# A two-layer trunk with experts: top two by eight-largest instructions, and a ring of 23 weight matrices opened in steps

## The chip, the cores and the metric

One core of a Trainium2 chip runs the whole kernel: TensorE (PE in the rows), VectorE (DVE), ScalarE (ACT), GpSimd (POOL), and SyncE (SP), whose queue issues every transfer. The metric is the device time of one execution in microseconds (us). The kernel before takes 1189.0 us, the median of three runs (1187.51 to 1193.46).

## The reference

There are two layers on 256 tokens of width 1024, all in float32. Each layer has a mixer sublayer (three token mixers on one input projection, merged by gates, then one output projection and a layer norm) and a mixture of experts. The expert part is what the change is about:

```python
group_logits = xt @ wg + bg
p_group = max(softmax(group_logits)); top_group = argmax(group_logits)
in_group = the 8 expert logits of that group            # 4 groups of 8 experts
top_val, top_idx = lax.top_k(in_group, 2)
w_top = softmax(top_val) * p_group
combine[t, e] = w_top at the two chosen experts, else 0
h_e = silu(x @ w_gate[e]) * (x @ w_up[e])               # 32 experts, each 1024 x 256
moe = sum over e of (h_e * combine[:, e]) @ w_down[e]   # 256 x 1024
h = layer_norm(ALPHA * h + moe)
```

An expert has three matrices of 1 MiB (gate, up, down), so that a layer reads 96 MiB of expert weights.

## The kernel before

**Weights.** `queue_weights` writes out one list of loads, in the order of use. `issue(pool)` takes the next one, gives it a 1 MiB tile (8 KiB in each partition) of a pool and puts its DMA on SP's queue; `done(key)` marks a matrix as used and issues the next load into the same pool. Four such tiles live for the whole kernel (`NBUF`), 13 are opened when the buffers of the mixers close (`NPRE`, `open_prefetch`), and five more (`NMORE`) when everything of the mixer sublayer has closed (`cr.close()`). SP works its queue in order: a load that waits for its tile holds back all behind it. At most eight loads are under way, since each waits for the eighth before it to land.

**The mixer's end.** Pools on the right side of the on-chip memory lie like a stack. The merge pool `gp` holds, among others, the mixers' outputs `o4`; on top lies `x`, with the transposed input `hT`. `merge_branch` works the three branches a, b and c; in the last one `between` closes `x`, opens a pool `out` there and begins to turn the merged result (`mix_turned`). `project_out` multiplies by `w_out` in two halves of 512 columns and starts the router's logits (`route`).

**The router.** `router` normalises, with `norm_scale` finding 1/sqrt by three Newton rounds of small VectorE operations. Beside it TensorE runs 26 multiplications whose result nobody uses (`warm`). Then the two best experts of each token are found: a maximum, an equality, a tie broken by position (`first`, three operations), the found one struck out, and the same again; `sel` is the sum of the two one-hots. Each of these steps is two instructions, one for each block of 128 tokens. Five small multiplications by triangles of ones turn `sel` into the token's place in each expert's list (`pos`), followed by `warm(6)`.

**The experts.** They are worked in quads of four: `QUADS` is 0, 1, 2, "x", 3 to 7, where "x" is a second turn of the expert with most tokens (99 MiB in all). For each quad `tokens` builds a 0/1 matrix `P` from `pos`, eight operations of 32 columns; `gather` multiplies by it and evicts to `xg`; `up` runs all gate and then all up matrices of the quad and calls `done` after each kind; `turn`, `down` and `combine` follow, while `weigh` (on POOL), `slots` and `slots_out` prepare the weights of the slots. `in_turn` keeps TensorE's order as written. Between the first quads POOL also applies the norm's gain and shift to the residual (`scaled`, eight operations); its two rows of 1024 values are broadcast to all partitions by four DMAs, issued before the router.

Of the kernel before, what the change touches and what calls it, by code (L numbers as in the profile page):

```python
# [20 lines left out]
KT = D // 128  # L21
# [43 lines left out]
def host_consts():  # L65
    p = np.arange(128)
    i64 = np.arange(64)
    j = (p % 64)[:, None]
    same = (p[:, None] // 64) == (p[None, :] // 64)
    S = {}  # L70
    S["ident"] = np.eye(128)
    S["rank"] = np.broadcast_to(p[None, :] + 1, (128, XCAP))
    S["down"] = np.broadcast_to(32 - np.arange(32)[None, :], (128, 32))
# [34 lines left out]
class Trunk:  # L108
# [35 lines left out]
    NBUF, NPRE, NMORE = 4, 13, 5  # L144
# [22 lines left out]
    def queue_weights(self):  # L167
        nc, A = self.nc, self.A

        def chunk(l, n):  # L170
            if n[:3] == "br_":
                c0, w, k, src = 512 * int(n[4]), 512, 4, A["w_br_" + n[3]][l]
            elif n[:-1] in WIDE:
                (a, c0), w, k = WIDE[n[:-1]], 512, 4
                src = A[a][l, 512 * int(n[-1]):512 * int(n[-1]) + 512]
            else:
                (c0, w), k, src = CH[n], 8, A["w_in"][l]

            def emit(t):
                return nc.sync.dma_start(t[:, :k * w].rearrange("p (k c) -> p k c", k=k),  # L180
                                         src.rearrange("(k p) c -> p k c", p=128)[:, :, c0:c0 + w])
            return (l, n), emit

        def expert(l, n, e):

            def emit(t):
                if e == "x":
                    src = A[n][l, bass.ds(self.heavy[l], 1)].rearrange("e (p k) f -> p (e k f)", p=128)
                else:
                    src = A[n][l, e].rearrange("(p k) f -> p (k f)", p=128)  # L190
                return nc.sync.dma_start(t, src)
            return (l, n, e), emit

        q, self.heavy = [], {}
        for l in range(DEPTH):
            q += [chunk(l, n) for n in ORDER]
            for quad in QUADS:
                q += [expert(l, n, e) for n in EXPERT for e in experts(quad)]
        self.wq = q[::-1]
        self.issue(self.wp)  # L200

    def issue(self, pool):
        if self.wq:
            key, emit = self.wq.pop()
            t = pool.tile([128, 2048], F32, name="w", tag="w", bufs=self.bufs[pool])
            self.last_weight = emit(t)
            self.wtiles[key] = t, pool
# [97 lines left out]
    def norm_scale(self, st, eps, centre=None):  # L305
# [3 lines left out]
        mv, rs, nm, v, tmp = (self.hp.tile([128, TB, w], F32, name=n, tag=n) for n, w in  # L309
                              (("ln_mv", 2), ("ln_rs", 1), ("ln_nm", 1), ("ln_v", 1), ("ln_tmp", 1)))  # L310
# [260 lines left out]
    def layer(self, l):  # L571
        tc, side = self.tc, dict(side="right")
        with ExitStack() as cl, ExitStack() as cr:
# [4 lines left out]
            hp = xp.enter_context(tc.tile_pool(name=f"x{l}", bufs=1, **side))  # L578
            with tc.tile_pool(name=f"mix{l}", bufs=1) as mp:
# [16 lines left out]
                self.hT = [hp.tile([128, KT, T], F32R, name=n) for n in ("hTh", "hTl")]  # L596
# [29 lines left out]
            po = ExitStack()  # L626

            def between():
                xp.close()
                pool = po.enter_context(tc.tile_pool(name=f"out{l}", bufs=1, **side))  # L630
                self.mixS = [pool.tile([128, 8, T], F32R, name=n) for n in ("mixh", "mixl")]
# [7 lines left out]
            with tc.tile_pool(name=f"h1_{l}", bufs=1, **side) as xp, tc.tile_pool(name=f"moe{l}", bufs=1, **side) as ep:  # L639
                self.moe(l, xp, ep, self.h)  # L640
# [475 lines left out]
    def o4(self, dt=F32R):  # L1116
        return [self.gp.tile([128, 4, T], dt, name="o4", tag="o4", bufs=self.NB["o4"]) for _ in range(2)]
# [156 lines left out]
    def project_out(self, l, po):  # L1274
# [16 lines left out]
        for c in range(2):  # L1291
            ps = [self.ps("pa") for _ in range(TB)]
            for i in range(2):
# [3 lines left out]
                if c == 1 and i == 0:  # L1297
                    for t in range(TB):
                        route(t, 0)
            cs = slice(512 * c, 512 * c + 512)  # L1300
# [8 lines left out]
    def router(self, l, ep, x, xc):  # L1309
# [46 lines left out]
        gm, pen, el, m1, m2, oh1, oh2, f = s(1), s(4), s(32), s(1), s(1), s(32), s(32), s(1)  # L1356
        es = self.small([128, TB, 32])
        for t in both:
            red(gm[t], lg[t][:, 0:4], axis=AX.X, op=OP.max)
# [44 lines left out]
        def heaviest(cmb):  # L1404
# [10 lines left out]
            ts(n, f1, -1.0, 32.0, op0=OP.mult, op1=OP.add)  # L1415
# [74 lines left out]
    def moe(self, l, xp, ep, h1):  # L1490
        nc, A = self.nc, self.A
        self.open_small(ep, 760)
# [16 lines left out]
        def tokens(q):  # L1509
# [3 lines left out]
            for t in range(TB):  # L1513
                if quad == "x":
                    nc.vector.tensor_scalar(P[:, t], rank, heavy[:, t, 0:1], self.rs[:, t], op0=OP.is_equal, op1=OP.mult)
                    continue
# [56 lines left out]
        def up(q):  # L1573
# [10 lines left out]
            if q == 0:  # L1584

                slots(0)
# [14 lines left out]
        def down(q):  # L1601
# [3 lines left out]
            for c in range(2):  # L1605
# [5 lines left out]
                y = [ep.tile([128, 512], F32R, name=n, bufs=2) for n in ("Yh", "Yl")]  # L1611
# [20 lines left out]
        heavy, past = heaviest(cmb)  # L1632
        tokens(1)
        with self.tc.issue_after(self.pool_last.ins):
            self.scaled(h1, *rows, nc.gpsimd)
# [6 lines left out]
        for q in range(nq + 1):  # L1642
            if q == 1:

                self.heavy[l] = nc.values_load(self.heaviest, engines=[mybir.EngineType.SP], min_val=0, max_val=NE - 1)
            if q < nq:
                self.in_turn(up, q)
            if q:
# [8 lines left out]
            if 3 <= q < 7:  # L1657
                c, t = divmod(q - 3, 2)
# [20 lines left out]
        rows = [[ep.tile([128, 512], F32, name=n, tag=n, bufs=2) for _ in range(2)] for n in ("Yh", "Yl")]  # L1679
# [52 lines left out]
```

## Time and profile before

| | us |
|---|---|
| runs: median, lowest, highest | 1189.0, 1187.51, 1193.46 |
| the profiled execution | 1191.11 |
| its span, first to last instruction | 1189.3 |

The profile is of one execution; its span and what lies around it (1.8 us) make up its time. Times in rows count from the first instruction. Layer 0 runs its experts from about 375 to 588 us, layer 1 from about 957 to 1170 us. PE is busy for 90% of the span, DVE 52%, ACT 37%, POOL 15%; 305.57 MB are moved. An engine's share says little here, since the stages have different limits.

### The profile page before, as it was taken

What the parts mean: (1) busy time and instruction counts of PE and PEld (TensorE: products, weight loads), DVE (VectorE), ACT (ScalarE), POOL (GpSimd) and SP (SyncE); (2) the same over time, 40 slices, a digit from 0 to 9 for tenths busy, and PEclk for the clock granted to TensorE, in tenths of its full rate; (3) what the DMA queues carried; (4) which work ended last, traced back from release to release, by engine and by line L of the source; (5) the groups of instructions that cost most, each with busy time, mean ns of one, the idle gap of its engine ahead of it and who ended that gap; (6) DMA issues with size and microseconds to landing.
All of it is one profiled execution on the core that took longest, in us unless ns stands there. A gap on an engine that the chain in (4) does not pass through costs nothing.

```text
span 1189.3 us, 21512 instructions
## 1 busy us (share of the span) xinstructions
PE 1065.1 (90%) x8846; PEld 770.8 (65%) x8846; DVE 615.1 (52%) x1404; ACT 444.8 (37%) x804; POOL 178.3 (15%) x160
## 2 busy tenths in 40 slices
PE   5899998999999899777689999899999999978775
PEld 4788976777777555334378889667777765634342
DVE  7787749366557234221177875665655563422214
ACT  4564553454444122111066545445444341211111
POOL 2411016001210300000024110430021131000001
PEclk9999998999999999888999999999999999997988
DMA  8632331358965999999983224215599579999994
GB/s 230 193 98 66 94 128 36 112 177 317 409 258 224 408 419 418 419 419 419 383 234 103 73 72 132 82 37 160 184 390 397 178 314 419 418 419 420 419 419 181
DMA packets 105282, 305.57 MB, mean 257 GB/s; under 512 B 21026, under 2 KB 48092, under 8 KB 79836
## 3 DMA queue, kind: packets, MB, share of 16 engines
q1 hardware_dynamic: 105180, 304.15, 67.9%
q8 instruction: 71, 1.16, 0.4%
q14 instruction: 31, 0.25, 0.1%
HBM read 303.08 MB, written 1.05 MB: 256 GB/s over the span
## 4 chain that ended last, share of the span: by engine, by line
PE 24%; DMA 15%; DVE 4%; ACT 3%; issue 2%; POOL 1%; SPq 1%; DVEq 0%; POOLq 0%
DMA w<-in_exp_w_gate_dram 5%; DMA w<-in_exp_w_down_dram 5%; DMA w<-in_exp_w_up_dram 3%; PE ps_pa L247 3%; PE ps_pa L246 3%; PE ps_pa L248 3%; PE ps_po L247 2%; PE ps_po L248 2%; PE ps_po L246 2%; DMA Yh<-in_ln_g_dram 2%; ACT wh L234 1%; PE ps_pa L1579 1%; DVE wl L235 1%; PE ps_pb L819 1%; PE ps_pm L1609 1%
## 5 line engine op out<-in xcount | busy, mean ns | idle before, releaser
L235 DVE TENSOR_TENSOR wl<-w,wh 128x1024 fp32r<-128x1024 f32 x150 | 187.9, 1253 | 156.9 <-ACT wh L234 156.1
L234 ACT CAST wh<-w 128x1024 fp32r<-128x1024 f32 x158 | 165.7, 1049 | 199.3 <-PE ps_pa L248 67.0
L1579 PE MATMUL ps_pa<-w,xg 128*32 128x256 f32 x2304 | 174.8, 431 | 60.6 <-DMA w<-in_exp_w_up_dram 35.1
L1579 PEld LDWEIGHTS ps_pa<-w,xg 128*32 128x32 f32 x2304 | 84.1, 123 | 145.8 <-DMA w<-in_exp_w_up_dram 46.3
L1590 DVE SCALAR_TENSOR_TENSOR hm<-ps_pa,ws,hm 128x256 f32<-128x256 f32 x18 | 8.7, 484 | 203.8 <-ACT hm L1589 203.6
L1589 ACT ACTIVATE hm<-ps_pa 128x256 f32<-128x256 f32 x18 | 6.9, 385 | 223.6 <-PE ps_pa L1579 223.6
L1609 PE MATMUL ps_pm<-w,hmT 128*32 128x512 f32 x576 | 70.9, 596 | 2.2 <-issue 1.3
L1529 PEld LDWEIGHTS ps_pm<-P,h1c 128*128 128x128 f32 x576 | 66.9, 192 | 2.9 <-ACT res L1331 1.1
L1529 PE MATMUL ps_pm<-P,h1c 128*128 128x128 f32 x576 | 67.8, 275 | 0.4
L1538 ACT ACTIVATE xg<-ps_pm,gb 128x128 f32<-128x128 f32 x72 | 33.0, 458 | 83.1 <-DVE xg L1536 82.9
L247 PE MATMUL ps_pa<-wl,hTh 128*128 128x512 f32 x144 | 58.5, 406 | 0.9 <-POOL wl L235 0.6
L246 PE MATMUL ps_po<-wh,hTh 128*128 128x512 f32 x144 | 58.2, 404 | 1.0 <-DVE mix L1260 0.6
L247 PE MATMUL ps_po<-wl,hTh 128*128 128x512 f32 x144 | 58.3, 405 | 0.9 <-POOL wl L235 0.6
L246 PE MATMUL ps_pa<-wh,hTh 128*128 128x512 f32 x144 | 58.2, 404 | 1.0 <-DVE mix L1260 0.5
L248 PE MATMUL ps_po<-wh,hTl 128*128 128x512 f32 x144 | 58.1, 404 | 0.0
L248 PE MATMUL ps_pa<-wh,hTl 128*128 128x512 f32 x144 | 57.8, 402 | 0.0
L1551 POOL TENSOR_TENSOR Pw<-P,small 128x128 f32<-128x128 f32 x32 | 12.4, 405 | 298.0 <-PE ps_pm L1558 220.0
L1262 POOL TENSOR_TENSOR mix<-mix,sg 128x512 f32<-128x512 f32 x16 | 28.3, 1788 | 153.0 <-DVE sg L1260 153.0
L246 PE MATMUL ps_pa<-hTh,wh 128*128 128x256 f32 (+1 forms) x168 | 49.4, 294 | 2.0 <-ACT wh L655 2.0
L1536 DVE TENSOR_SCALAR xg<-ps_pm,gb 128x128 f32<-128x128 f32 x72 | 29.5, 409 | 41.4 <-PE ps_pm L1529 32.4
L248 PE MATMUL ps_pa<-hTh,wl 128*128 128x256 f32 (+1 forms) x168 | 49.2, 293 | 0.7 <-DVE wl L235 0.5
L248 PE MATMUL ps_po<-hTh,wl 128*128 128x256 f32 (+1 forms) x168 | 49.1, 292 | 0.5 <-DVE wl L235 0.5
(468 smaller groups left out, 2282.6 us busy)
## 6 DMA issues: line engine op xcount, KB each, us to landing
w<-in_exp_w_gate_dram SPq DMA_DIRECT2D x66, 1024.0 KB
w<-in_exp_w_up_dram SPq DMA_DIRECT2D x66, 1024.0 KB
w<-in_exp_w_down_dram SPq DMA_DIRECT2D x66, 1024.0 KB
w<-in_w_in_dram SPq DMA_DIRECT2D x58, 1024.0 KB
w<-in_w_out_dram SPq DMA_DIRECT2D x8, 1024.0 KB
w<-in_w_br_a_dram SPq DMA_DIRECT2D x4, 1024.0 KB
w<-in_w_br_b_dram SPq DMA_DIRECT2D x4, 1024.0 KB
w<-in_w_br_c_dram SPq DMA_DIRECT2D x4, 1024.0 KB
```

What stands on the lines that cost most here:

```text
L234: nc.scalar.copy(v(hi), raw)
L235: engine.tensor_tensor(v(lo), raw, v(hi).bitcast(F32), op=OP.subtract)
L246: mm(ps, a[0], b[0], start=start, stop=False, skip_group_check=True)
L247: mm(ps, a[0], b[1], start=False, stop=False, skip_group_check=True)
L248: mm(ps, a[1], b[0], start=False, stop=stop, skip_group_check=True)
L1262: nc.gpsimd.tensor_tensor(mv, mv, sg[t], op=OP.add)
L1529: nc.tensor.matmul(ps[:, 128 * k:128 * k + 128], xc[:, t, 4 * h + k], Ps[q][:, t], start=(t == 0), stop=(t == 1))
L1536: nc.vector.tensor_scalar(xg[:, k], o, g, b, op0=OP.mult, op1=OP.add)
L1538: nc.scalar.activation(xg[:, k], o, AF.Identity, scale=g, bias=b)
L1551: self.pool_last = nc.gpsimd.tensor_tensor(e(Pw[:, t]), e(P[:, t]), w, op=OP.mult)
L1579: nc.tensor.matmul(pg[32 * e:32 * e + 32, FF * n:FF * n + FF], xgs[q][k // 4][:, k % 4, 32 * e:32 * e + 32], w[:, FF * k:FF * k + FF], sta ...
L1609: nc.tensor.matmul(ps[32 * e:32 * e + 32], hmT[:, i, 32 * e:32 * e + 32], w[:, D * i + 512 * c:D * i + 512 * c + 512], start=(i == 0), sto ...
```

## The change

1. **Ring.** The five late tiles are opened in steps: two when branch c is merged (`o4` now has a pool of its own, `o`, on top of `x`, that closes first), two after the last multiplication by `w_out` (`free` closes `x`; the turned result now lies in the tiles of `hT`), one at `cr.close()`. One load, the gate matrix of expert 3, is taken out of the list and goes to a tile of its own (`once`), so that 23 matrices fit before the first is used. That tile is not used again for weights: the tiles of `Y` lie there afterwards.
2. **Rows.** The norm's two rows are one entry of the weight list, behind quad 1, and `scaled` is called at quads 2 and "x".
3. **Top two.** `max` gives the eight largest values of a row at once. A score `sc` of one or two values (with the position breaking ties), and a second `max`, replace the two searches; `sel` is one comparison, and the one-hots are made later, in `weights`.
4. **P** is built by two operations of 256 columns in place of eight of 32.
5. **Norm.** The three Newton rounds become one round of third order and one Newton round: nine operations in place of twelve.

```diff
-    NBUF, NPRE, NMORE = 4, 13, 5
+    NBUF, NPRE = 4, 13
+        def rows(l):
+            def emit(t):
+                for i, n in enumerate(("ln1_g", "ln1_b")):
+                    self.bcast_row(t[:, D * i:D * i + D], A[n][l], D)
+            return (l, "rows"), emit
             for quad in QUADS:
                 q += [expert(l, n, e) for n in EXPERT for e in experts(quad)]
+                if quad == 1:
+                    q += [rows(l)]
+            self.once[l] = q.pop(q.index(next(x for x in q if x[0] == (l, EXPERT[0], 3))))
...
-        if pool is self.wp or (self.wq and self.wq[-1][0][0] == key[0]):
+        if pool is self.wp or pool in self.bufs and (self.wq and self.wq[-1][0][0] == key[0]):
...
-        ts(v, v, -0.5, None, op0=OP.mult)
+        ts(v2, v, -0.5 * 27 / 512, None, op0=OP.mult)
...
-        for _ in range(3):
-            for t in range(TB):
-                ts(tmp[:, t], rs[:, t], rs[:, t], v[:, t], op0=OP.mult, op1=OP.mult)
-            for t in range(TB):
-                ts(rs[:, t], tmp[:, t], 1.5, rs[:, t], op0=OP.add, op1=OP.mult)
+        for t in range(TB):
+            ts(tmp[:, t], rs[:, t], rs[:, t], v[:, t], op0=OP.mult, op1=OP.mult)
+        nc.vector.scalar_tensor_tensor(tmp, tmp, -10.0 / 3, tmp, op0=OP.add, op1=OP.mult)
+        for t in range(TB):
+            ts(rs[:, t], tmp[:, t], 5.0, rs[:, t], op0=OP.add, op1=OP.mult)
+        for t in range(TB):
+            ts(tmp[:, t], rs[:, t], rs[:, t], v2[:, t], op0=OP.mult, op1=OP.mult)
+        for t in range(TB):
+            ts(rs[:, t], tmp[:, t], 1.5 * 3 / 8, rs[:, t], op0=OP.add, op1=OP.mult)
...
             self.merge_branch(l, "c", between)
-            with po:
-                self.project_out(l, po)
+            oc.close()
+            self.open_prefetch(f"more{l}a", 2)
+            def free():
+                xp.close()
+                self.open_prefetch(f"more{l}b", 2)
+            self.project_out(l, free)
             cr.close()
-            self.open_prefetch(f"more{l}", self.NMORE)
+            self.open_prefetch(f"more{l}c", 1)
...
         for t in both:
-            red(m1[t], el[t], axis=AX.X, op=OP.max)
-        first(oh1, el, m1, 32)
+            nc.vector.max(top[t], el[t])
+        m1, m2 = ([x[:, i:i + 1] for x in top] for i in range(2))
         for t in both:
-            stt(el[t], oh1[t], -3e38, el[t], op0=OP.mult, op1=OP.add)
+            stt(c[t], el[t], m2[t], down, op0=OP.is_ge, op1=OP.mult)
         for t in both:
-            red(m2[t], el[t], axis=AX.X, op=OP.max)
-        first(oh2, el, m2, 32)
+            stt(sc[t], el[t], m2[t], c[t], op0=OP.is_gt, op1=OP.add)
+        for t in both:
+            nc.vector.max(rank2[t], sc[t])
...
-            tt(sel[:, t], oh1[t], oh2[t], op=OP.add)
+            ts(sel[:, t], sc[t], rank2[t][:, 1:2], None, op0=OP.is_ge)
...
+                for i, oh in enumerate((oh1, oh2)):
+                    ts(oh[t], sc[t], rank2[t][:, i:i + 1], None, op0=OP.is_equal)
...
-        rows = [[ep.tile([128, 512], F32, name=n, tag=n, bufs=2) for _ in range(2)] for n in ("Yh", "Yl")]
-        for r, n in zip(rows, ("ln1_g", "ln1_b")):
-            for c in range(2):
-                self.bcast_row(r[c], A[n][l, 512 * c:512 * c + 512], 512)
+        yp = yc.enter_context(self.tc.tile_pool(name=f"once{l}", bufs=1, side="right"))
+        key, emit = self.once[l]
+        self.wtiles[key] = yp.tile([128, 2048], F32, name="w"), yp
+        emit(self.wtiles[key][0])
...
-                for e in range(4):
-                    i = nc.vector.tensor_scalar(P[:, t, CAP * e:CAP * e + CAP], rank[:, 0:CAP], pos[:, t, 4 * quad + e:4 * quad + e + 1],
-                                            self.rs[:, t], op0=OP.is_equal, op1=OP.mult)
-                    self.last_P = i.ins
+            nc.vector.tensor_tensor(P.rearrange("p t (e s) -> p t e s", s=CAP),
+                                    pos[:, :, 4 * quad:4 * quad + 4, None].to_broadcast([128, TB, 4, CAP]),
+                                    rank[:, None, None, 0:CAP].to_broadcast([128, TB, 4, CAP]), op=OP.is_equal)
+            self.last_P = nc.vector.tensor_tensor(P, P, self.rs.to_broadcast([128, TB, 128]), op=OP.mult).ins
...
-        with self.tc.issue_after(self.pool_last.ins):
-            self.scaled(h1, *rows, nc.gpsimd)
...
+            if q in (2, 3):
+                r = self.w(l, "rows")
+                self.scaled(h1, *([r[:, D * i + 512 * c:D * i + 512 * c + 512] for c in range(2)] for i in range(2)), nc.gpsimd,
+                            [q - 2])
+                if q == 3:
+                    self.done(l, "rows")
```

Three engines get another order. On SP, at the end of layer 0's mixers, this is the queue of loads before, each with the engines or the earlier transfer (DMAHW) that it waits for; it begins with the last load that waits for a tile of `w_out`:

```order
L191 DMA w<-in_exp_w_up_dram 128x2048 [waits DMAHW4_49,DVE_49]
L191 DMA w<-in_exp_w_up_dram 128x2048 [waits DMAHW5_49,PE_49,Activation_49]
L191 DMA w<-in_exp_w_up_dram 128x2048 [waits DMAHW6_49]
L191 DMA w<-in_exp_w_up_dram 128x2048 [waits DMAHW7_49]
L191 DMA w<-in_exp_w_down_dram 128x2048 [waits DMAHW0_49]
L191 DMA w<-in_exp_w_down_dram 128x2048 [waits DMAHW1_49]
L297 DMA Yh<-in_ln_g_dram 128x512 [waits DMAHW2_49]
L297 DMA Yh<-in_ln_g_dram 128x512 [waits DMAHW3_49]
L297 DMA Yl<-in_ln_b_dram 128x512 [waits DMAHW4_49]
L297 DMA Yl<-in_ln_b_dram 128x512 [waits DMAHW5_49]
L191 DMA w<-in_exp_w_down_dram 128x2048 [waits DMAHW6_49,PE_49]
```

And now, from the first of the two tiles that `o4` leaves (a wait for PE) to the rows:

```order
L191 DMA w<-in_exp_w_gate_dram 128x2048 [waits DMAHW1_49,PE_49]
L191 DMA w<-in_exp_w_gate_dram 128x2048 [waits DMAHW2_49]
L191 DMA w<-in_exp_w_up_dram 128x2048 [waits DMAHW3_49,DVE_49]
L191 DMA w<-in_exp_w_up_dram 128x2048 [waits DMAHW4_49,DVE_49]
L191 DMA w<-in_exp_w_up_dram 128x2048 [waits DMAHW5_49,DVE_49]
L191 DMA w<-in_exp_w_up_dram 128x2048 [waits DMAHW6_49,DVE_49]
L191 DMA w<-in_exp_w_down_dram 128x2048 [waits DMAHW7_49,PE_49]
L191 DMA w<-in_exp_w_down_dram 128x2048 [waits DMAHW0_49]
L191 DMA w<-in_exp_w_down_dram 128x2048 [waits DMAHW1_49,PE_49,Activation_49]
L191 DMA w<-in_exp_w_gate_dram 128x2048 [waits DMAHW2_49]
L191 DMA w<-in_exp_w_down_dram 128x2048 [waits DMAHW3_49,PE_49]
L308 DMA w<-in_ln_g_dram 128x1024 [waits DMAHW4_49,PE_49]
```

The five loads that stood together behind the wait for PE and ACT are now two, two and one, the lone gate matrix stands behind them, and the rows come behind the first load that needs a used expert matrix to go.

On DVE, the router of layer 0 before, from the first maximum to `P` (x2: one instruction for each block of tokens):

```order
L1365 TENSOR_REDUCE small<-small 128x1 x2
L1347 SCALAR_TENSOR_TENSOR small<-small,const 128x32 x2
L1349 TENSOR_REDUCE small<-small 128x1 x2
L1352 TENSOR_SCALAR small<-small 128x32 x2
L1368 SCALAR_TENSOR_TENSOR small<-small 128x32 x2
L1370 TENSOR_REDUCE small<-small 128x1 x2
```

It goes on with the same three steps for the second expert, `sel` and `pos`. Now, from the first `max` to `P`:

```order
L1391 MAX small<-small 128x8 x2
L1395 SCALAR_TENSOR_TENSOR small<-small,const 128x32 x2
L1397 SCALAR_TENSOR_TENSOR small<-small 128x32 x2
L1399 MAX small<-small 128x8 x2
L1402 TENSOR_SCALAR sel<-small 128x32 x2
L1414 SCALAR_TENSOR_TENSOR small<-ps_pb,sel 128x64
L1546 TENSOR_TENSOR P<-small,const 128x256
L1549 TENSOR_TENSOR P<-P,ln_rs 128x256
```

Ten steps up to `sel` have become five, and `P` is two instructions right behind `pos`.

On POOL, the first quads of a layer before (`Pw` is the weighted `P` of a quad, two operations a quad; `res` is the residual that `scaled` works on):

```order
L1551 TENSOR_TENSOR Pw<-P,small 128x128 x2
L359 TENSOR_TENSOR res<-res,Yh 128x512 x4
L360 TENSOR_TENSOR res<-res,Yl 128x512 x4
L1551 TENSOR_TENSOR Pw<-P,small 128x128 x4
L1547 TENSOR_TENSOR Pw<-P,small 128x128 x2
```

And now:

```order
L1580 TENSOR_TENSOR Pw<-P,small 128x128 x4
L375 TENSOR_TENSOR res<-res,w 128x512 x4
L376 TENSOR_TENSOR res<-res,w 128x512 x4
L1580 TENSOR_TENSOR Pw<-P,small 128x128 x2
L1576 TENSOR_TENSOR Pw<-P,small 128x128 x2
```

All eight operations on the residual have moved behind the `Pw` of quad 1 and stand ahead of that of quad 2. TensorE's and ACT's orders are the same as before.

## Rows read from the trace of the kernel before

**Rows 1.** The page's 40 slices of the span: busy tenths of the DMA engines
```profile
DMA  8632331358965999999983224215599579999994
```
**Rows 2.** The chain of waits, layer 1's end: start us, us, what
```profile
1009.03 20.03 DMA w<-in_exp_w_gate_dram
...
1170.30 3.62 PE ps_pm L1609 x20
...
1175.56 5.27 DMA Yh<-in_ln_g_dram
```
**Rows 3.** Stretches: from:to, us, PE busy (x), PEclk, DMA share, GB/s
```profile
388.47:587.78 199.31, 163.61 (x1714) 0.93 1.01 416
970.83:1170.25 199.42, 167.19 (x1713) 0.91 1.00 411
976.83:1165.50 188.67, 156.73 (x1606) 0.91 1.01 419
956.55:970.83 14.28, 13.56 (x131) 1.00 0.93 371
970.83:976.83 6.00, 6.00 (x88) 1.00 0.99 365
956.55:958.55 2.00, 2.00 (x11) 1.00 0.47 86
923.90:956.55 32.65, 31.45 (x160) 1.00 0.41 145
```
**Rows 4.** SP's queue: start us, us, engine, line, transfer, count
```profile
956.55 1.28 SPq L191 DMA_DIRECT2D w<-in_exp_w_up_dram  x3
970.83 0.80 SPq L191 DMA_DIRECT2D w<-in_exp_w_down_dram  x2
```
**Rows 5.** TensorE in order of time: start us, us, line, tiles, shape, count
```profile
598.13 4.31 PE L348 MATMUL ps_pa<-bits 128*128 128x512 bf16 x13 [2.40 <-issue]
...
923.49 0.39 PE L248 MATMUL ps_po<-wh,o 128*128 128x512 f32 x1
951.77 0.40 PE L248 MATMUL ps_po<-wh,mixl 128*128 128x512 f32 x1
956.31 4.48 PE L348 MATMUL ps_pa<-bits 128*128 128x512 bf16 x20
961.32 0.19 PE L1377 MATMUL ps_pb<-sel,bits 128*128 128x32 bf16 x1 [0.52 <-DVE sel L1374]
961.52 1.46 PE L348 MATMUL ps_po<-bits 128*128 128x512 bf16 x6
963.03 4.19 PE L1529 MATMUL ps_pm<-P,h1c 128*128 128x128 f32 x32
967.15 7.11 PE L1579 MATMUL ps_pa<-w,xg 128*32 128x256 f32 x128
974.48 3.74 PE L1529 MATMUL ps_pm<-P,h1c 128*128 128x128 f32 x32
1001.79 0.44 PE L1558 MATMUL ps_pm<-const,Pw 128*128 128x128 f32 x2
```
**Rows 6.** VectorE, a row of the start, then layer 1's router
```profile
21.40 0.42 DVE L432 TENSOR_TENSOR d<-d 128x256 f32<-128x256 f32 x1
...
954.65 0.46 DVE L322 TENSOR_SCALAR ln_tmp<-ln_rs,ln_v 128x1 f32<-128x1 f32 x2
955.27 0.45 DVE L322 TENSOR_SCALAR ln_tmp<-ln_rs,ln_v 128x1 f32<-128x1 f32 x2
958.72 0.30 DVE L1365 TENSOR_REDUCE small<-small 128x1 f32<-128x32 f32 x2
961.08 0.32 DVE L1374 TENSOR_TENSOR sel<-small 128x32 bf16<-128x32 f32 x2
961.97 1.75 DVE L1518 TENSOR_SCALAR P<-const,small,ln_rs 128x32 f32<-128x32 f32 x8
```
**Rows 7.** POOL, the residual's first four operations in layer 1
```profile
973.08 4.96 POOL L359 TENSOR_TENSOR res<-res,Yh 128x512 f32<-128x512 f32 x4 [5.96 <-DMA Yh<-in_ln_g_dram]
```

More of the change, by code (lines that the diff above doesn't have):

```diff
@@ L72, in host_consts @@
     S["rank"] = np.broadcast_to(p[None, :] + 1, (128, XCAP))
-    S["down"] = np.broadcast_to(32 - np.arange(32)[None, :], (128, 32))
+    S["down"] = np.broadcast_to((32 - np.arange(32)[None, :]) / 64, (128, 32))
     S["neg"] = np.full((128, 4), -1e30)
@@ L192, in expert @@
             return (l, n, e), emit
-        q, self.heavy = [], {}
+        def rows(l):
[3 more added lines that the diff above has]
+            return (l, "rows"), emit
+        q, self.heavy, self.once, self.last_issue = [], {}, {}, None
         for l in range(DEPTH):
@@ L625, in layer @@
             self.merge_branch(l, "b")
-            po = ExitStack()
             def between():
-                xp.close()
-                pool = po.enter_context(tc.tile_pool(name=f"out{l}", bufs=1, **side))
-                self.mixS = [pool.tile([128, 8, T], F32R, name=n) for n in ("mixh", "mixl")]
+                self.mixS = [hp.tile([128, 8, T], F32R, name=n, tag=n) for n in ("hTh", "hTl")]
                 self.mix_turned(0)
             self.merge_branch(l, "c", between)
-            with po:
-                self.project_out(l, po)
+            oc.close()
[4 more added lines that the diff above has]
+            self.project_out(l, free)
             cr.close()
-            self.open_prefetch(f"more{l}", self.NMORE)
-            with tc.tile_pool(name=f"h1_{l}", bufs=1, **side) as xp, tc.tile_pool(name=f"moe{l}", bufs=1, **side) as ep:
-                self.moe(l, xp, ep, self.h)
+            self.open_prefetch(f"more{l}c", 1)
+            with tc.tile_pool(name=f"h1_{l}", bufs=1, **side) as xp, tc.tile_pool(name=f"moe{l}", bufs=1, **side) as ep, \
+                    ExitStack() as yc:
+                self.moe(l, xp, ep, yc, self.h)
     def dn_decay(self, l, mp):
@@ L1116, in o4 @@
     def o4(self, dt=F32R):
-        return [self.gp.tile([128, 4, T], dt, name="o4", tag="o4", bufs=self.NB["o4"]) for _ in range(2)]
+        return [self.op.tile([128, 4, T], dt, name="o4", tag="o4", bufs=self.NB["o4"]) for _ in range(2)]
     def dump_oT(self, l, n):
@@ L1272, in mix_turned, with project_out @@
             self.split_act(*[x[:, k:k + 2].rearrange("p k t -> p (k t)") for x in self.mixS], ps)
-    def project_out(self, l, po):
+    def project_out(self, l, free):
         nc, A = self.nc, self.A
@@ L1299, in project_out @@
                         route(t, 0)
+            if c:
+                free()
             cs = slice(512 * c, 512 * c + 512)
@@ L1354, in first @@
                     stt(out[t], e[t], f[t], other, op0=OP.is_lt, op1=OP.mult)
-        gm, pen, el, m1, m2, oh1, oh2, f = s(1), s(4), s(32), s(1), s(1), s(32), s(32), s(1)
+        gm, pen, el, oh1, oh2, f, top, sc, rank2 = s(1), s(4), s(32), s(32), s(32), s(1), s(8), s(32), s(8)
         es = self.small([128, TB, 32])
+        c = [es[:, t] for t in both]
         for t in both:
@@ L1512, in tokens @@
             rank, quad = self.cst("rank"), QUADS[q]
-            for t in range(TB):
-                if quad == "x":
+            if quad == "x":
+                for t in range(TB):
                     nc.vector.tensor_scalar(P[:, t], rank, heavy[:, t, 0:1], self.rs[:, t], op0=OP.is_equal, op1=OP.mult)
-                    continue
-                for e in range(4):
-                    i = nc.vector.tensor_scalar(P[:, t, CAP * e:CAP * e + CAP], rank[:, 0:CAP], pos[:, t, 4 * quad + e:4 * quad + e + 1],
-                                            self.rs[:, t], op0=OP.is_equal, op1=OP.mult)
-                    self.last_P = i.ins
+                return
+            nc.vector.tensor_tensor(P.rearrange("p t (e s) -> p t e s", s=CAP),
+                                    pos[:, :, 4 * quad:4 * quad + 4, None].to_broadcast([128, TB, 4, CAP]),
+                                    rank[:, None, None, 0:CAP].to_broadcast([128, TB, 4, CAP]), op=OP.is_equal)
+            self.last_P = nc.vector.tensor_tensor(P, P, self.rs.to_broadcast([128, TB, 128]), op=OP.mult).ins
         def gather(q):
@@ L1584, in up @@
             if q == 0:
-                slots(0)
+                with self.tc.issue_after(self.latest(nc.tensor)):
+                    slots(0)
                 slots_out(0)
@@ L1631, in moe @@
         weigh(0)
-        heavy, past = heaviest(cmb)
+        with self.tc.issue_after(self.last_P):
+            heavy, past = heaviest(cmb)
         tokens(1)
-        with self.tc.issue_after(self.pool_last.ins):
-            self.scaled(h1, *rows, nc.gpsimd)
         if l + 1 < DEPTH:
@@ L1643, in moe @@
             if q == 1:
-                self.heavy[l] = nc.values_load(self.heaviest, engines=[mybir.EngineType.SP], min_val=0, max_val=NE - 1)
+                with self.tc.issue_after(self.last_issue.ins):
+                    self.heavy[l] = nc.values_load(self.heaviest, engines=[mybir.EngineType.SP], min_val=0, max_val=NE - 1)
             if q < nq:
                 self.in_turn(up, q)
+            if q == 0:
+                yc.close()
+                yp = yc.enter_context(self.tc.tile_pool(name=f"y{l}", bufs=1, side="right"))
+            if q in (2, 3):
[4 more added lines that the diff above has]
+                    self.done(l, "rows")
             if q:
@@ L1678, in moe @@
             return
-        rows = [[ep.tile([128, 512], F32, name=n, tag=n, bufs=2) for _ in range(2)] for n in ("Yh", "Yl")]
+        rows = [[yp.tile([128, 512], F32, name=n, tag=n, bufs=2) for _ in range(2)] for n in ("Yh", "Yl")]
         for r, n in zip(rows, ("ln2_g", "ln2_b")):
```

22 lines of the change are left out of this document (12 added, 10 removed).

## The prediction, made before the changed kernel ran

> **What bounds the kernel now.** The 40 slices come first [rows 1]: two long stretches with the DMA engines at 9 tenths, each the expert part of a layer. The chain of waits says what the second is made of: from 1009 us until the last matmuls of the down product at 1170.30 every link that holds is a weight transfer [rows 2]. The stretches give its rate: 419 GB/s over 188.67 us, the DMA share at 1.01 while PE is busy for 156.73 us only [rows 3]. At that rate 1 MiB takes 1.0486 / 419 = 2.50 us. So in an expert part only two things count: how many bytes are still to come once the tiles begin to go round, and when that happens. I read that moment from SP's queue: after the loads at 956.55, which `cr.close()` frees, the next two start at 970.83 [rows 4], when the gate half of the first `up` is done (it starts at 967.15 and takes 7.11 in all [rows 5]). Call it the first release. From there to the end of the stream layer 0 takes 199.31 and layer 1 199.42 [rows 3], so I work with layer 1 and count it twice. The rest, mixers and end, the change hardly touches: the last chain ends in the rows of the closing norm, 5.27 us of DMA [rows 2].
>
> **The ring.** Before, 22 matrices and 1 MiB of norm rows are issued ahead of the first release; now 22 and the lone gate matrix are, and the rows come behind. That is 23 MiB either way, so the earlier tiles don't lower what is issued afterwards (99 + 1 - 23 = 77 MiB in both). What they alter is how much of the 23 has landed. Before, 956.55 to 970.83 ran at 371 GB/s, 14.28 x 371 = 5.30 MB or 5.05 MiB of the 6 issued there; 0.95 MiB was still under way at the release, worth 2.4 us. Now two tiles open at about 923.9, behind the last multiplication that reads `o`, and two at 952.2, behind the last by `w_out` [rows 5]. The DMA engines have room there: 145 of 419 GB/s in use from 923.90 to 956.55 [rows 3], 8.5 MiB free in 32.65 us. Then only the second pair and two further matrices are left, 4 MiB from 952.2, landed at 952.2 + 1.6 + 4 x 2.5 = about 964. All 23 lie in memory before the release: -2.4 us a layer.
>
> The queue also ran thin after the release: 970.83 to 976.83 at 365 GB/s, 6.00 x (1 - 365 / 419) = 0.77 us [rows 3]. Now three tiles are given back by the gate matrices at once (the lone one isn't), and four by the up matrices some 3.6 us later, so the loads that follow wait for none: -0.75, nothing to -0.77. Against it, the DMA engines now stand idle before the release and have to start again. The nearest row is the start at 956.55: 86 GB/s in its first 2.00 us, 2.00 x (1 - 86 / 419) = 1.6 us lost [rows 3]. The bounds are 0 (the small transfers never let it stop) and the 1.64 that the 371 GB/s of the whole 14.28 give; I take 1.6. [...]
>
> **The first release.** What leads to it is TensorE's chain. The norm loses a Newton round, 955.27 - 954.65 = 0.62, less one operation of about 0.19: -0.43 us. The search for the two best takes 10 pairs from 958.72 to 961.40, 0.27 each; five remain, 1.34 [rows 6]. No row shows the eight-largest instruction. Its bounds are a pair of reductions of the same 32 columns, 0.30, and eight of these, 2.4; it reads the operand of one reduction, so I take 0.30. [...] So `sel` would be ready at 961.40 - 0.43 - 1.34 = 959.6. But TensorE works its queue as written, and the last 20 of the 26 unused multiplications run from 956.31 to 960.79 [rows 5]. The triangles start at 960.8 in place of 961.32: of 1.77 us gained on VectorE 0.5 counts.
>
> `P` follows 0.65 us behind the triangles' start (961.97 against 961.32). Eight operations took 1.75; two of 256 columns, priced by a row of that shape, 0.42 each [rows 6], are done at 962.3, ahead of the second unused run, which ends at 960.8 + 0.2 + 1.46 = 962.5 [rows 5]. The first gather took 4.19, the next 3.74: it waited 0.45 for the second half of `P` [rows 5]. It now runs 962.5 to 966.2. The bounds for the pair are 0.84 and the old 1.75 (its operands are spread copies of short rows, which that row doesn't show); at 1.75 the gather ends at 966.9. I take the first. `up` then starts 0.95 us earlier, and so does the release: at 969.9.
>
> **Work that is only moved.** The four one-hot operations of `weights` stand behind `P` now, beside the first half of the gather. POOL's eight operations on the residual take 2 x 4.96 us [rows 7]; the rows are issued at about 970.0 and land at 976.4 behind one matrix, so they end near 986.4, and what POOL does next is wanted by TensorE at 1001.79 [rows 5], 1000 or so in the new kernel: nothing lost, with 13 us of cover. SP's queue has the rows ahead of 75 matrices, the same bytes as before. The shorter norm at layer 0's end lies beside 4.31 us of unused multiplications [rows 5], and the last one beside the 5.27 us of the rows: nothing. At the kernel's start no such cover stands; 0 to 0.43, I take 0.3.
>
> **Sum.** A layer: -0.95 - 2.4 - 0.75 + 1.6 = -2.5; twice, with 0.3: -5.3 us. The profiled execution, 1189.3 of span and 1.8 around it, would come to 1185.8; it lies 2.1 above the median of the runs, so the median goes from 1189.0 to 1183.7.
>
> **The rivals.**
> - *The tiles count in full.* If four matrices fetched earlier shortened the stream by their 10.0 us a layer, the time would be 1189.0 - 20.0 = 1169. For it: the free 8.5 MiB. Against it: the same 23 MiB stand ahead of the release. 0.04.
> - *The router counts in full.* If the unused run let go earlier, the release would come 2.1 us sooner (0.43 + 1.34 + the rest of the gather), 1.2 a layer more than forecast: 1181.3. Against it: TensorE's order has all 20 in front. 0.13.
> - *Little is left.* The refill after the release is as thin as before (slots come back in the same two lots) and the gather still waits for `P`: -0.3 - 2.4 + 1.6 = -1.1 a layer, -2.5 in all, 1186.5. For it: the slump lies just where the first tiles return. 0.15.
> - *The lone matrix is late: slower.* It is issued last, and all four gates are read at once. If the four early tiles were not landed when `cr.close()` comes, six matrices lie in line: 956.55 + 1.6 + 6 x 2.5 = 973.2 in place of 966.2, and each us costs one in each layer: 7.0 - 2.5 = +4.5, 1189.0 + 8.7 = 1197.7. It decides from about 968.7, two matrices behind the forecast. The 145 GB/s speak against it. With it goes the dear end of the eight-largest instruction: 2 x 2.1 us later, `sel` at 963.8, +0.5 a layer, 1189.7. 0.08 together.
>
> **How the numbers follow.** The forecast has 0.60. About 0.5% of 1189, 6 us, is what a measurement of this kernel can tell from no change: the line is 1183.0, and the forecast lies 0.7 short of it, its own range being 1181.5 to 1186. Faster: 0.25 of its 0.60, 0.04 of the first rival, 0.11 of the second: 0.40. Slower: 0.05 of the last. The same: 0.55. The range reaches from 1178.5 (the second rival with most of the restart not lost) to 1189.0 (nothing gained).
>
> **What would show it.** Right: the triangles start straight behind the unused run; the first gather takes 3.7 us without a pause; the DMA engines stand idle from about 964 to 1.6 us after the release; that comes near 969.9, and from it to the end of the stream it is 198 us and not 199.4; POOL's residual work ends ahead of the `Pw` that TensorE wants. Wrong: a first `up` that waits for a transfer, a stream with gaps later on (the forecast has none), or a mixer stage whose length differs.

## The result and the profile after

The changed kernel takes 1182.51 us (median of five, 1180.36 to 1183.15) where the kernel before took 1188.48 (median of five) beside it. The measured ratio is 0.9932, 95% interval 0.9914 to 0.9950. It is not the quotient of these two medians, which is 0.9950, at the upper end of the interval; it agrees with the kernel before's medians in the later sessions, 1190.5 to 1190.7 us. So the change is 0.5 to 0.7% faster, at or just beyond the line of 0.5% that the forecast stopped short of, and the time lies 1.2 us below the 1183.7 forecast. The profiled execution took 1180.36 us, its span 1178.6; it is the quickest of the five, and that of before (1191.11) is slower than four of its five, so the spans differ by 10.7 us and the medians by 6.0.

Nearly every step that was worked out is in the trace. TensorE, in layer 1 (start us, us, line, tiles, shape, count):

```profile
951.65 4.48 PE L364 MATMUL ps_pa<-bits 128*128 128x512 bf16 x20
955.97 0.18 PE L1405 MATMUL ps_pb<-sel,bits 128*128 128x32 bf16 x1
957.58 3.81 PE L1558 MATMUL ps_pm<-P,h1c 128*128 128x128 f32 x32
961.32 7.11 PE L1608 MATMUL ps_pa<-w,xg 128*32 128x256 f32 x128
993.69 0.44 PE L1587 MATMUL ps_pm<-const,Pw 128*128 128x128 f32 x2
```

The triangles start 4.32 us behind the start of the unused run, before 5.01 [rows 5], and without a wait; the gather takes 3.81, not 4.19; `up` starts 9.67 behind the unused run and not 10.84. VectorE shows why:

```profile
953.92 0.31 DVE L1391 MAX8 small<-small 128x8 f32<-128x32 f32 x2
955.03 0.38 DVE L1402 TENSOR_SCALAR sel<-small 128x32 bf16<-128x32 f32 x2
956.55 0.42 DVE L1546 TENSOR_TENSOR P<-small,const 128x256 f32<-128x256 f32 x1
957.01 0.42 DVE L1549 TENSOR_TENSOR P<-P,ln_rs 128x256 f32<-128x256 f32 x1
```

A pair of eight-largest instructions takes 0.31, like a pair of reductions [rows 6]; `sel` is ready at 955.4, half a us ahead of TensorE; `P` is two operations of 0.42. SP's queue:

```profile
947.54 4.67 SPq L191 DMA_DIRECT2D w<-in_exp_w_down_dram  x3
952.26 0.42 SPq L191 DMA_DIRECT2D w<-in_exp_w_gate_dram  x1
964.99 0.33 SPq L191 DMA_DIRECT2D w<-in_exp_w_down_dram  x1
```

The first release is at 964.99, 13.34 us behind the unused run's start; before it was 970.83 - 956.31 = 14.52 [rows 4, 5]. So it is 1.18 us earlier in its layer (0.95 forecast). The stretches (from:to, us, busy time of PE, PEld, DVE, ACT and POOL, then PEclk, DMA share, GB/s):

```profile
960.00:966.00 6.00, 6.00 (x101) 4.08 (x103) 3.34 (x20) 3.12 (x5) 0.85 (x2) 1.00 0.05 10
964.99:970.99 6.00, 6.00 (x88) 4.45 (x81) 1.61 (x4) 0.38 (x1) 0.76 (x2) 1.00 0.81 288
972.99:1152.99 180.00, 150.64 (x1569) 84.76 (x1573) 42.26 (x96) 25.67 (x53) 13.81 (x21) 0.92 1.01 426
964.99:1159.81 194.82, 164.91 (x1714) 93.63 (x1706) 45.80 (x104) 27.49 (x57) 16.36 (x24) 0.92 0.99 416
```

The DMA engines stand nearly idle from 960 to the release; the first 6 us behind it lose 6.00 x (1 - 288 / 426) = 1.9 us to the restart and to what was left of the slump. But one thing nobody asked for is there: the stream runs at 426 GB/s and not at 419 [rows 3]. From the release to the last of the down matmuls (1159.81) it is 194.82 us; before, 199.47. Of these 4.65 us the ring was to give 1.55; 77 MiB at the higher rate, 77 x (2.503 - 2.461) = 3.2, make up the rest.

POOL does the residual's work ahead of the `Pw` that TensorE wants at 993.69, with 11 us to spare:

```profile
971.21 5.34 POOL L375 TENSOR_TENSOR res<-res,w 128x512 f32<-128x512 f32 x4 [1.56 <-DMA w<-in_ln_g_dram]
976.51 4.99 POOL L376 TENSOR_TENSOR res<-res,w 128x512 f32<-128x512 f32 x4
981.45 0.77 POOL L1580 TENSOR_TENSOR Pw<-P,small 128x128 f32<-128x128 f32 x2
```

And at the start of the kernel something is late by 2.6 us: the first matmul of a 128x72 tile, first here and then before:

```profile
28.74 0.34 PE L257 MATMUL ps_pa<-hTh,wh 128*72 128x256 f32 x1 [1.84 <-ACT wh L678]
26.17 0.34 PE L246 MATMUL ps_pa<-hTh,wh 128*72 128x256 f32 x1 [2.05 <-ACT wh L655]
```

### The profile page after: what moved, and what is told of

It is laid out like the page before. It is cut to its first block, busy times and chain, and to the rows that moved or that the text cites. A ratio compares the mean times of both kernels' runs of the same rounds, so it can differ in the third digit from the quotient of the medians.

```text
span 1178.6 us, 21364 instructions
## 1 busy us (share of the span) xinstructions
PE 1063.1 (90%) x8846; PEld 771.1 (65%) x8846; DVE 603.7 (51%) x1281; ACT 445.0 (38%) x804; POOL 179.2 (15%) x160
## 3 DMA queue, kind: packets, MB, share of 16 engines
q8 instruction: 71, 1.16, 0.4%
## 5 line engine op out<-in xcount | busy, mean ns | idle before, releaser
L257 PE MATMUL ps_pa<-wh,hTh 128*128 128x512 f32 x176 | 71.3, 405 | 2.0 <-ACT hTh L250 0.7
L257 PE MATMUL ps_po<-wh,hTh 128*128 128x512 f32 x176 | 71.3, 405 | 2.0 <-ACT hTh L250 0.7
L258 PE MATMUL ps_po<-wl,hTh 128*128 128x512 f32 x176 | 71.1, 404 | 0.9 <-POOL wl L246 0.6
L258 PE MATMUL ps_pa<-wl,hTh 128*128 128x512 f32 x176 | 71.1, 404 | 0.9 <-POOL wl L246 0.6
L259 PE MATMUL ps_pa<-wh,hTl 128*128 128x512 f32 x176 | 70.8, 402 | 0.2 <-DVE hTl L251 0.2
L259 PE MATMUL ps_po<-wh,hTl 128*128 128x512 f32 x176 | 70.7, 401 | 0.2 <-DVE hTl L251 0.2
L1639 PEld LDWEIGHTS ps_pm<-w,hmT 128*32 128x32 f32 x576 | 22.0, 109 | 42.2 <-issue 29.6
```

The source lines that it names most:

```text
L257: mm(ps, a[0], b[0], start=start, stop=False, skip_group_check=True)
L258: mm(ps, a[0], b[1], start=False, stop=False, skip_group_check=True)
L259: mm(ps, a[1], b[0], start=False, stop=stop, skip_group_check=True)
L1639: nc.tensor.matmul(ps[32 * e:32 * e + 32], hmT[:, i, 32 * e:32 * e + 32], w[:, D * i + 512 * c:D * i + 512 * c + 512], start=(i == 0), sto ...
```

## The experiments

Ratios are to the kernel before on the same chip, whose median was 1190.5 to 1190.7 us there; 0.001 is 1.2 us. Like the ratio above they are not quotients of medians, which differ from them by up to 0.0009. The first four ask for the rate, the norm, the unused run and the ring.

**The kernel before again**, no edit.

> The kernel before, unchanged, for a second profile of it. In the first pair of profiles the weight stream ran at 419 GB/s before the change and at 426 after it, worth 77 x (2.503 - 2.461) = 3.2 us a layer. Theory A (the rate differs from one execution to the next, whatever the kernel): this profile, or some other of the old kernel's order, shows a rate other than 419, and the time of the profiled execution goes with it by about 0.9 us for each GB/s (6.4 us for 7). Theory B (the change raises the rate, say by its deeper queue): the rate is 419 within 1. The ratio to before is 1.000 within 0.002 by either.

1.0005 (0.9993 to 1.0017), at 419 GB/s. No other rate, so chance is out as far as two profiles go.

**The old norm in the changed kernel.**

```diff
-        nc.vector.scalar_tensor_tensor(tmp, tmp, -10.0 / 3, tmp, op0=OP.add, op1=OP.mult)
...
+        for _ in range(3):
```

> The changed kernel with the three Newton rounds of before. Theory A (the shorter norm moved VectorE's work at the kernel's start beside GpSimd's second subtraction of 128x1024, and so costs 1.0 us there; at the other three places it is hidden, because TensorE's unused run holds the router): 1.0 us faster than the changed kernel, and the first merged matmuls come as early as before (the fourth weight load of 128x72 columns at 26.2 us and not at 28.7). Theory B (the prediction's: the norm is worth 0.3 us at the start): 0.3 us slower than the changed kernel, 1182.8.

0.9961 (0.9946 to 0.9977): slower than the changed kernel by some 3.5 us, against both theories. The start is early (26.58 us), as theory A has it, but the stream runs at 419 GB/s again:

```profile
974.38:1154.38 180.00, 149.62 (x1533) 83.14 (x1533) 42.03 (x96) 25.64 (x53) 13.82 (x21) 0.92 1.01 419
```

So the rate hangs on something that came with the norm.

**A shorter unused run.**

```diff
-        self.warm(26)
+        self.warm(23)
-            self.warm(6)
+            self.warm(5)
```

> The changed kernel with 23 and 5 unused multiplications in place of 26 and 6 in the router. Theory A (TensorE's written order holds the router, 0.56 us a layer behind VectorE's selection, and each us of the first release is a us of the end): the triangles start at VectorE's pace, 0.5 us earlier, the gather 0.6; 1.0 to 1.3 us faster in all, about 1181.4. Theory B (the bytes alone set the end, as the DMA engines stand idle there anyway): within 0.2 us of the changed kernel. Theory C (TensorE's clock falls with three fewer multiplications): the granted clock of the first gather is under 1.00 and the time is 2 us or more longer.

0.9926 (0.9911 to 0.9942), not to be told from the changed kernel; the time alone doesn't rule theory A out. TensorE:

```profile
953.32 3.84 PE L364 MATMUL ps_pa<-bits 128*128 128x512 bf16 x17
957.00 0.18 PE L1405 MATMUL ps_pb<-sel,bits 128*128 128x32 bf16 x1
958.68 3.81 PE L1558 MATMUL ps_pm<-P,h1c 128*128 128x128 f32 x32 [0.24 <-DVE P L1549]
962.42 7.78 PE L1608 MATMUL ps_pa<-w,xg 128*32 128x256 f32 x128
```

The triangles come 3.68 behind the run's start and `up` 9.10, as theory A says; the clock stays at 1.00, so theory C falls. But `up` now takes 7.78: its weight loads wait 0.5 us for the last gate matrix, and the release is at 13.07, only 0.27 earlier. The lone matrix of the fourth rival is next in line.

**The ring alone**: the kernel before with items 1 and 2 of the change.

> The kernel before with the ring and the rows of the changed one, but the old search, P and norm. Theory A (the prediction's sum: the ring gives 2.4 + 0.75 - 1.6 = 1.55 us a layer, the router and P 0.95 to 1.2): 3.1 us faster than before, 1185.4, with the release to the stream's end 1.5 us shorter at the same rate. Theory B (the change raises the stream's rate by its ring): the rate is 426 here too, and the time 3.1 + 6.4 = 9.5 us less, 1179. Theory C (the ring gives nothing): 1188.5.

0.9977 (0.9966 to 0.9989), 2.7 us for the 3.1 of theory A, at 419 GB/s; from the release to the last down matmul it is 198.31 us in layer 1, 1.16 less than before, where 1.55 was forecast. Theory B, that the ring raises the rate, falls.

```profile
965.76:1164.07 198.31, 168.06 (x1714) 93.94 (x1706) 56.88 (x140) 27.46 (x57) 16.01 (x24) 0.91 0.99 408
```

**The place of the tiles.** What the kernels at 426 have and those at 419 lack is the new norm's extra small tile, `ln_v2`. It takes 32 bytes in each partition, below the weight tiles, and moves all of them but the lone one: the first from byte 15328 (480 modulo 512) to 15360 (0 modulo 512). Four kernels move them with one, one, two and eight tiles of 32 bytes that nobody uses. The first is the kernel before:

```diff
-                              (("ln_mv", 2), ("ln_rs", 1), ("ln_nm", 1), ("ln_v", 1), ("ln_tmp", 1)))
+                              (("ln_mv", 2), ("ln_rs", 1), ("ln_nm", 1), ("ln_v", 1), ("ln_pad", 1), ("ln_tmp", 1)))
```

> The kernel before, with one unused tile of 32 bytes per partition in the pool of the norm's small tiles: it does no work, and moves every weight tile from an address that is 32 modulo 64 (15328 for the first) to a multiple of 512 (15360). In the profiles so far the stream runs at 426 GB/s in both kernels with the new norm and at 419 in the four others; the new norm has one small tile more, which moves the weight tiles by the same 32 bytes. Theory A (the place of the tiles sets the rate): 426 GB/s, the release to the last down 3.3 us shorter a layer, 6.5 us less in all, ratio 0.9945. Theory B (something else of the new norm or of the router does): 419 GB/s and ratio 1.000.

0.9941 (0.9924 to 0.9958): the kernel before, with nothing but 32 bytes more, is about as fast as the changed one.

```profile
975.07:1155.07 180.00, 148.01 (x1557) 83.26 (x1561) 46.96 (x132) 25.47 (x53) 9.95 (x20) 0.93 1.01 426
```

> The changed kernel with one unused tile of 32 bytes among the norm's small tiles, so that the weight tiles lie at 32 modulo 64 again. Theory A (place): 419 GB/s, the release to the last down 198.2 us in layer 1 and not 194.8, 6.5 us slower than the changed kernel, ratio to before 0.9955 or so, as the changed kernel with the old norm had (0.9961). Theory B (the norm's own work): 426 GB/s and 0.993.

0.9994 (0.9983 to 1.0005): the changed kernel, moved by 32, is no faster than the one before. The rate is that of theory A, and the loss against the changed kernel is 7.4 us for its 6.5; but the 0.9955 that it names is missed by 4.6 us. Most of that is the distance to the changed kernel with the old norm (0.9961), 3.9 us at the same rate: the new norm's work, to which a later section comes.

```profile
976.67:1156.67 180.00, 150.18 (x1533) 84.40 (x1533) 42.31 (x97) 25.77 (x53) 13.96 (x21) 0.91 1.01 419
```

> The changed kernel with two unused tiles of 32 bytes: the weight tiles lie at 64 modulo 512. Theory A1 (a place at a multiple of 64 bytes is enough): 426 GB/s, and the time of the changed kernel, 0.993. Theory A2 (it must be a multiple of 128 or more, up to 512): a rate below 426, and with 419 a ratio of 0.9955.

0.9976 (0.9966 to 0.9986), 420 GB/s: theory A2 by the rate, with the time 2.5 us above its 0.9955; a multiple of 64 isn't enough.

```profile
977.10:1157.10 180.00, 149.43 (x1541) 84.72 (x1545) 42.19 (x97) 25.78 (x53) 13.87 (x21) 0.91 1.01 420
```

Last, with eight such tiles:

> The changed kernel with eight unused tiles of 32 bytes: the weight tiles lie at 256 modulo 512. Theory A1 (a multiple of 256 is enough): 426 GB/s and the changed kernel's time, 0.993. Theory A2 (it must be a multiple of 512): 419 to 422 GB/s, 5 us slower, 0.997.

0.9934 (0.9922 to 0.9946), 426 GB/s: a multiple of 256 is (128 wasn't tried).

```profile
972.89:1152.89 180.00, 150.49 (x1569) 85.02 (x1573) 42.24 (x96) 25.71 (x53) 13.77 (x21) 0.92 1.01 426
```

The five places side by side: 419 and 420 GB/s at 32, 64 and 480 modulo 512, 426 at 0 and 256. The loss of 7 GB/s doesn't follow the distance from the last multiple of 256: a start at 480 lies 480 - 256 = 224 bytes behind it, one at 32 lies 32, and both run at 419. So that the place sets the rate is shown, and how the 1.7% comes about is not.

**The tiles opened late.**

```diff
-            self.open_prefetch(f"more{l}a", 2)
...
             cr.close()
-            self.open_prefetch(f"more{l}c", 1)
+            for n, k in zip("abc", (2, 2, 1)):
+                self.open_prefetch(f"more{l}{n}", k)
```

> The changed kernel with its five late tiles opened together when everything of the mixer sublayer has closed, as before the change; the lone gate matrix is issued behind them. Theory A (the prediction's fourth rival gives the price of a late lone matrix): six matrices stand in line at that moment, the last lands at 0.2 + 1.6 + 6 x 2.46 = 16.6 us behind the start of the unused run, where the first `up` would start at 9.7: 6.9 us a layer, 13.9 in all, ratio 1.005, with PE waiting for a gate matrix at the first `up`. Theory B (opening the tiles early gives nothing, since the bytes ahead of the release are the same): 0.993.

0.9956 (0.9943 to 0.9969), some 2.9 us slower than the changed kernel, not 13.9; the two intervals overlap a little. The edit did less than meant. The loads waited here for the last reader of the memory under their tile, not for the line that opens the pool: in the changed kernel the last multiplication that reads `o` ends at 919.25 us, and the first load into a tile of `o4` goes out at 919.28. These are the loads into the two tiles of `o4`, first in the changed kernel and then here:

```profile
919.28 0.81 SPq L191 DMA_DIRECT2D w<-in_exp_w_gate_dram  x2
943.30 0.86 SPq L191 DMA_DIRECT2D w<-in_exp_w_up_dram  x2
```

Only these two tiles got their loads later. The four tiles that came behind them in the queue now come ahead and get theirs as their memory falls free, from 922.96 to 942.88 us (in the changed kernel, whose router is 1.35 us earlier, from 921.62 to 941.55). `up` stopped for 0.27 us at a gate matrix. The full price of a late matrix was not measured.

**The norm's work at the start.** Three kernels keep the tiles at a multiple of 512. With the three Newton rounds and one unused tile:

> The changed kernel with the three Newton rounds of before and one unused tile of 32 bytes, so that the weight tiles stay at a multiple of 512: the new norm's work taken back without its move of the tiles. Theory A (the shorter norm lets GpSimd's second subtraction of the start overtake VectorE's, and costs 2 to 3 us there): ratio about 0.990, 2 to 3 us faster than the changed kernel (0.9932), and in the profile the first 128x72 matmul at about 26.2 us and not 28.7, at 426 GB/s. Theory B (the norm's work costs nothing or gains 0.3 us, and the move of the tiles is its whole effect): 0.993.

0.9899 (0.9884 to 0.9915), 1178.12 us: the best of all, 3.9 us faster than the changed kernel, with the first 128x72 matmul at 26.04 us and 426 GB/s, as theory A has it. With the second subtraction of the first input matrix on VectorE, then with the shorter unused run as well:

```diff
-    POOLED = {"cq.0", "cq.1", "gla00.0", "dn_gate1.1"}
+    POOLED = {"cq.0", "gla00.0", "dn_gate1.1"}
```

> The changed kernel with the second subtraction of the first input matrix on VectorE in place of GpSimd, in both layers: VectorE's two-operand work at the start can't be held by it. Theory A (as above): 2 to 3 us faster than the changed kernel, about 0.991, with no operation of VectorE over 1.5 us between 16 and 22 us. Theory B (the 1.25 us that VectorE takes for it come out as late): 0.993. At 426 GB/s by either.

> The last kernel with 23 and 5 unused multiplications in the router in place of 26 and 6. By theory A of both, 2 to 3 us from the start and 0.2 to 0.6 us a layer from the earlier release: 1178.5, ratio 0.990. If neither counts 0.993.

0.9928 (0.9916 to 0.9941) and 0.9917 (0.9904 to 0.9929). The first 128x72 matmul is early in both (26.82, 27.14), yet they gain 0.5 and 1.8 us only: the first has the 0.993 of theory B. What happens at the start is plain. VectorE and POOL of the changed kernel, and TensorE:

```profile
13.83 1.99 DVE L441 SCALAR_TENSOR_TENSOR d<-d 128x256 f32<-128x256 f32 x1
16.19 3.45 DVE L251 TENSOR_TENSOR hTl<-d,hTh 128x512 fp32r<-128x512 f32 x2
20.81 1.28 DVE L251 TENSOR_TENSOR hTl<-d,hTh 128x512 fp32r<-128x512 f32 x2
```

```profile
16.50 2.59 POOL L246 TENSOR_TENSOR wl<-w,wh 128x1024 fp32r<-128x1024 f32 x1 [0.53 <-ACT wh L245]
```

```profile
19.70 0.58 PE L258 MATMUL ps_pm<-hTl,wh 128*128 128x256 f32 x1 [1.55 <-DVE hTl L251]
```

```profile
19.70:24.10 4.40, 4.40 (x20) 4.40 (x21) 2.85 (x8) 1.14 (x3) 0.00 (x0) 0.50 0.78 175
```

The pair of `hTl` takes 3.45 us where the next takes 1.28: of its halves the first takes 0.68 and the second 2.85, which ends at 19.64, 0.55 behind the end of POOL's subtraction (19.09). TensorE stands idle until 19.70 and then works at a granted clock of 0.50 for 4.4 us. With the old norm (the kernel at 0.9899) VectorE is first:

```profile
15.78 1.37 DVE L251 TENSOR_TENSOR hTl<-d,hTh 128x512 fp32r<-128x512 f32 x2
17.98 1.83 DVE L438 SCALAR_TENSOR_TENSOR d<-d 128x256 f32<-128x256 f32 x1
```

```profile
17.16 2.38 POOL L246 TENSOR_TENSOR wl<-w,wh 128x1024 fp32r<-128x1024 f32 x1 [1.15 <-ACT wh L245]
```

There the operation that is long beside POOL's subtraction (1.83 us; 0.41 at 20.47 in the changed kernel, with POOL at rest) is one that TensorE doesn't wait for. The kernel before has the same, beside POOL's subtraction from 17.30 to 19.67:

```profile
18.12 1.84 DVE L427 SCALAR_TENSOR_TENSOR d<-d 128x256 f32<-128x256 f32 x1
```

In each of these an operation of VectorE ends just behind POOL's subtraction: the pair of `hTl` 0.55 us behind it in the changed kernel and also in the second profile of the kernel before (there 3.54 us long), the operation above 0.27 in the kernel at 0.9899 and 0.29 in the first profile of the kernel before. Not all of VectorE's work is longer: two operations of 128x256 that read `ps_pb` took 0.98 us beside the subtraction (17.08 us, the kernel at 0.9899) and 0.98 without it (19.57, the changed one). Why only some are is not shown. Which one it is changes from one execution to the next: of the profiles with the old norm five are early and one late (29.18, the kernel before in its second profile), of those with the new norm, its subtraction left on POOL, one is early (26.42) and five late.

The clock of 0.50 is not the pause's doing, and the early kernel pays for it too. From:to as above, two stretches of the changed kernel and then two of the one at 0.9899:

```profile
17.60:24.20 6.60, 5.05 (x24) 4.76 (x24) 5.05 (x9) 1.24 (x3) 1.49 (x1) 0.50 0.75 164
27.50:30.70 3.20, 1.69 (x12) 1.44 (x13) 2.57 (x8) 2.12 (x4) 0.00 (x0) 1.00 0.07 14
```

```profile
17.30:20.50 3.20, 3.20 (x17) 3.20 (x16) 3.17 (x5) 0.92 (x2) 2.24 (x1) 0.50 0.63 130
27.50:30.70 3.20, 3.20 (x17) 3.20 (x16) 0.69 (x1) 0.00 (x0) 0.00 (x0) 0.50 0.05 7
```

In both the clock falls while TensorE is busy: a matmul of 128x256 goes from 0.28 us to 0.41 at 17.52 in the late kernel, whose pause begins at 18.15, and to 0.40 at 17.18 in the early one. The late kernel has one long stretch at 0.50, the early one two short ones, the second of them just after its early 128x72 matmuls have begun. The first triangle multiplication of layer 0 shows what is left of the late start of 2.70 us (28.74 against 26.04), in the changed kernel and in the other:

```profile
379.31 0.18 PE L1405 MATMUL ps_pb<-sel,bits 128*128 128x32 bf16 x1
378.20 0.18 PE L1400 MATMUL ps_pb<-sel,bits 128*128 128x32 bf16 x1
```

It is 1.11 us; and at the end the two spans are 1178.6 and 1178.2.

## Why the prediction was right, and where it was wrong

| part | forecast | measured, from |
|---|---|---|
| ring and rows | -3.1 us | -2.7, ring alone |
| router and `P` | -1.9 | -1.9, old norm less ring alone (0.9961, 0.9977) |
| norm's work | -0.3 | +3.9, changed kernel against 0.9899 |
| place of the weight tiles | not seen | -7.0, 32 bytes more in the kernel before (7.4 in the changed kernel: 0.9994, 0.9932) |
| sum | -5.3 | -7.7; the changed kernel itself 0.9932, -8.1 |

*The ring and the first release came out as worked.* The same 23 MiB ahead of the release, 0.95 MiB of them no longer outstanding, a restart of about 1.6 to 1.9 us, TensorE's written order holding the router: all are in the rows. Two terms were within 0.4 us a layer: the stream of the ring alone gave 1.16 for 1.55, the first release came 1.18 earlier for 0.95. The -1.9 of the router and `P` is a difference of two ratios whose intervals overlap; the 1.18 a layer of the trace, 2.4 in all, is the better witness. The first rival (10 us a layer) is out. So is the thin one as a whole (1.1 a layer), since the gather doesn't wait; but the 1.16 lies midway between the 1.55 forecast and the 2.4 - 1.6 = 0.8 of a refill as thin as before, and no run tells restart and refill apart. The second, a router that counts in full, is out for the reason given, and a further one that the short unused run showed: behind the order stands the lone matrix.

*Two steps failed, with opposite signs.* The first is the opening one, "The stretches give its rate: 419 GB/s", taken over unchanged: nothing was said on where the tiles lie, although the new norm needs one small tile more (`v2` in the diff). It holds 7 us, more than any other term. Three pairs of kernels that differ by one unused tile alone give 7.0 to 7.4: the two of the table, and the old norm in the changed kernel (0.9961 at 419 GB/s, 0.9899 at 426). The second is "At the kernel's start no such cover stands; 0 to 0.43, I take 0.3": a shorter chain on VectorE was taken for a gain, and what it would meet on POOL was not looked at, though the kernel before already shows an operation of 1.84 us beside POOL's subtraction; the late start is the sign that the prediction named itself, a mixer stage whose length differs. Together they make -3.1 where the forecast had -0.3; so that the time was met to 1.2 us is luck as much as working: two large errors against each other.

*What stays open.* The norm's work cost 3.9 us between the changed kernel and the one at 0.9899, with intervals that only touch (0.9884 to 0.9915 against 0.9914 to 0.9950). A second pair, at 419 GB/s, gives 3.9 too, with intervals apart: the old norm 0.9961 (0.9946 to 0.9977, tiles at 480), the changed kernel moved by 32 bytes 0.9994 (0.9983 to 1.0005, tiles at 32). So the cost is measured twice; where it arises is not. The collision at the start is shown, and moves the start by 2 to 3 us in the profiles; but of 2.70 us only 1.11 were left at layer 0's router and 0.4 at the end, in the second pair both profiles start early (26.58 and 26.42), and with the subtraction on VectorE the start was early and the median hardly better. A profile shows one execution of each, so it can't settle what the medians lose. That the collision is the cause of the 3.9 is not shown.

## What to carry to other kernels

When a change adds or drops any small buffer, look where the big DMA targets come to lie before crediting its work; here 32 bytes moved the time by 7.0 to 7.4 us, the whole ring by 2.7. Undo a change's parts one by one at the same addresses, or the parts that move memory take the credit of those that don't. And a chain made shorter on one engine starts its next work earlier (here by 0.2 to 0.3 us, 9.97 for 10.18 and 10.30): see what runs beside it then on the other engines (here a pair of 1.28 us took 3.45 beside a subtraction on POOL), and follow a delay to the end of its stage before pricing it; here more than half of it was gone by layer 0's router.

## What the runs showed of the hardware that was not expected

- The stream of 1 MiB loads (8 KiB in each partition) ran at 419 GB/s into tiles at 32 or 480 modulo 512 bytes, 420 at 64, 426 at 0 and 256: 1.7%, the same in both layers and in both profiles of the kernel before.
- A VectorE pair of 128x512 subtractions took 3.45 us in place of 1.28 with POOL's 128x1024 subtraction beside it. Which of the two came first changed between executions of the same kernel (26.17 and 29.18 us for the first 128x72 matmul of the kernel before).
- The eight largest of 32 columns cost as much as one reduction of them: 0.31 us the pair, the reductions 0.30.
